# Gates of layer 1 in the ring of input tiles, the last two gate projections block by block, layer 1's weights loaded ahead

## The chip, the cores and the metric

The kernel runs on one core of a Trainium2 chip. The metric is the device time of one execution in microseconds (us). TensorE (PE) multiplies matrices into PSUM; VectorE (DVE) and ScalarE (ACT) do elementwise work and read PSUM; GpSimd (POOL) does elementwise work in SBUF; SyncE (SP) issues all of the kernel's DMA transfers, in order.

## The reference

Two encoder layers over 2048 tokens of width 1024. Each layer projects its modulated input, mixes it along time, multiplies the result with SiLU of gate columns, projects back and ends in a scaled residual and a layer norm. Layer 0 mixes with HGRN2 heads and RWKV7 heads; layer 1 with a gated linear recurrence (RG-LRU), which is the part that matters here:

```python
else:
    u = h @ od_w_in[o]
    xC, gC = jnp.split(u, 2, axis=-1)
    hC = rglru_branch(xC, od_conv_w[o], ...)   # conv of 4 taps, gates r and i, scan along time
    y = (hC * jax.nn.silu(gC.astype(f32))).astype(x.dtype) @ od_w_out[o]
x = layer_norm(DEEPNORM_ALPHA * x + (1.0 + gate[:, None]) * y, ln_g[l], ln_b[l])

# in rglru_branch
log_a = -C_POW * gate_r * jax.nn.softplus(-lam.astype(f32))
a = jnp.exp(log_a)
u = jnp.sqrt(-jnp.expm1(2.0 * log_a)) * (gate_i * xc)
_, h = lax.associative_scan(combine, (a, u), axis=1)
```

## The kernel before

Every product in f32 is made from three passes: both operands are split into a high part and a rest (split, L366 to L368: ACT casts the high part at L367, DVE or POOL subtracts the rest at L368), and mm3 (L430 to L433) issues low times high, high times high, high times low. A projection of 128 output columns is thus 24 matmuls of 128x512 for each half-block of 512 tokens.

Each layer runs over two super-blocks of 1024 tokens (sb = 0, 1), each of two half-blocks (b = 0, 1). The stages come as mix0_0, out0_0, mix0_1, out0_1, then mix1_0, out1_0, mix1_1, out1_1. A mix stage projects, mixes, and writes the mixed rows to o_dr in DRAM; its gate_steps (L551) projects the eight gate tiles k, multiplies each with its rows of o_dr, and writes the product to m_dr. An out stage (out_proj, L482) reads m_dr back as stationary operands (raw_mx), multiplies with the output weights (wo) and norms; beside it the next stage's inputs are prepared (out0_1 and out1_0 read them from x1_dr).

In mix1 (L1251) the eight conv inputs are projected two by two (pp_c, tiles u_c), and mix_c (L1092) treats each of four groups g: four conv steps into xc on ACT and DVE, a split of xc, 48 matmuls of the block-diagonal gates into pg_c, ACT's sigmoids gr and gi, and then, over the whole group at once, tanh, exp, square and sqrt on ACT and products on DVE, and at the end DVE's two scans into hc_c and their stores to o_dr. The tiles hc_c are of the tag c_o with two buffers; the gate tiles go of layer 1 have the same tag. The gate projections follow the groups in the program; a scheduler orders PE, ACT, DVE, POOL and SP by priority, which falls in program order but for blocks raised by high_priority, and fills PE's waits of mix_c with projections that are ready. In mix0 PE's order is written out by hand (manual_schedule), and the gates come at the end of it.

A gate's two half-blocks go to two PSUM blocks of the tag mm (two buffers), are copied by ACT to go (L574), put through SiLU (L564), multiplied on DVE with oi, the rows of o_dr (L568, loaded at L577), and stored to m_dr (L586). The last gate of a stage is not stored but split into tail tiles, half-block by half-block. The ring up (L101, 11 buffers of 515 f32 a partition) holds conv inputs u_c, oi, the tail tiles and gb, the broadcast output gate (L485).

Weights come through load_w, raw with two buffers, then high and low parts with four; load_w raises its priority by ahead. load_wo reads wo into tiles freed by the stage: in layer 0 two loads into the buffer of the tag sgi, which the last gate tile had, two into that of lr, which the gate before it had. An out stage's first matmul therefore stands behind the last gate's copy, SiLU, product and split, the load of wo, and wo's split.

Of the kernel before, what the change touches and what calls it, by code (L numbers as in the profile page):

```python
# [13 lines left out]
F32 = mybir.dt.float32  # L14
# [9 lines left out]
P = 128  # L24
D = 1024
KT = 8
BLK = 512
SBT = 1024
# [40 lines left out]
def tile_encoder(  # L69
# [47 lines left out]
    tp = _Cur()  # L117
    ps = ctx.enter_context(tc.tile_pool(name="ps", bufs=1, space=PSUM))
# [291 lines left out]
    def load_w(src, name, nk=KT, raws=None, ahead=0):  # L410
        with tc.high_priority(offset=ahead):
            return split_w(src, name, nk, raws)
# [17 lines left out]
    def mm3(pt, ah, al, bh, bl, first, last):  # L430
        nc.tensor.matmul(pt, ah, bl, start=first, stop=False)  # L431
        nc.tensor.matmul(pt, ah, bh, start=False, stop=False)  # L432
        nc.tensor.matmul(pt, al, bh, start=False, stop=last)  # L433

    def proj_steps(src, name, hs, evac, w=None):

        wh, wl = w or load_w(src, name)
        for b in range(2):
            pt = ps.tile([P, BLK], F32, name=f"pp_{name}_{b}", tag="mm", bufs=2)
            for k in range(KT):  # L440
                mm3(pt, wh[k], wl[k], hs[0][b][k], hs[1][b][k], k == 0, k == KT - 1)
                if k in (1, 3, 5):
                    yield
            evac(b, pt)
            yield

    def proj(*a):
        for _ in proj_steps(*a):
            pass

    def proj_start_steps(ws, hs):
# [96 lines left out]
            norm(j)  # L548
            after(j)

    def gate_steps(l, sb, hs, wsrc, ct0, order, tail, tags):  # L551


        def half(name, dt=F32):
            return up.tile([P, BLK + 3], dt, name=f"{name}_{l}_{sb}", tag="u")[:, 0:BLK]

        for n, k in enumerate(order):
            t0 = sb * SBT
            last = k == order[-1]
            go, oi = {}, {}  # L560

            def silu_mul(bs):
                for b in bs:
                    silu = nc.scalar.activation(go[b], go[b], AF.Silu)  # L564
                if l == 0:
                    ln_exp_after(silu)
                for b in bs:
                    nc.vector.tensor_mul(go[b], go[b], oi[b])  # L568

            def evac(b, pt):  # L570
                if b == 0:
                    g2 = tp.tile([P, 2, BLK], F32, name=f"go_{l}_{sb}_{k}", **tags[n % len(tags)])
                    go.update({0: g2[:, 0], 1: g2[:, 1]})
                nc.scalar.copy(go[b], pt)  # L574
                for j in (b,) if last else range(2) if b else ():
                    oi[j] = half(f"oi{k}_{j}")
                    nc.sync.dma_start(oi[j], o_dr[l][k, :, t0 + j * BLK : t0 + (j + 1) * BLK])  # L577
                if last:
                    silu_mul((b,))
                    hl = [half(f"m{i}_{b}", F32R) for i in range(2)]  # L580
                    split(hl[0], hl[1], go[b])
                    tail.append(hl)
                elif b:
                    silu_mul((0, 1))
                    for j in range(2):
                        nc.sync.dma_start(m_dr[l][k, :, t0 + j * BLK : t0 + (j + 1) * BLK], go[j])  # L586

            yield from proj_steps(wsrc[ct0(k)], f"g{l}_{sb}_{k}", hs, evac)


    a_state = [None] * 4
# [498 lines left out]
    c_state = [None] * 8  # L1090

    def mix_c(g, sb, us):  # L1092
        wh, wl = load_w(w_gate[g], f"wg{sb}_{g}")
        nm = f"c{g}_{sb}"
        xc = tp.tile([P, 2, SBT], F32, name=f"xc_{nm}", tag="c_x")
        gr = tp.tile([P, 2, SBT], F32, name=f"gr_{nm}", tag="c_gr")
        gi = tp.tile([P, 2, SBT], F32, name=f"gi_{nm}", tag="c_gi")
        for b in range(2):
            ls = slice(b * BLK, (b + 1) * BLK)
            xh = []  # L1100
            xl = []
            for i in range(2):
                ct = 2 * g + i
                u = us[i][b]
                x_ = xc[:, i, ls]
                nc.scalar.activation(
                    x_, u[:, 3 : BLK + 3], AF.Identity, scale=V("conv_w", 24 + ct), bias=V("conv_b", ct)
                )
                for w in range(3):
                    nc.vector.scalar_tensor_tensor(  # L1110
                        out=x_, in0=u[:, w : w + BLK], scalar=V("conv_w", 8 * w + ct), in1=x_,
                        op0=ALU.mult, op1=ALU.add,
                    )
                hi = tp.tile([P, BLK], F32R, name=f"xh{i}_{nm}_{b}", tag=f"c_h{i}", bufs=2)
                lo = tp.tile([P, BLK], F32R, name=f"xl{i}_{nm}_{b}", tag=f"c_l{i}", bufs=2)
                split(hi, lo, x_)
                xh.append(hi)
                xl.append(lo)
            for i in range(2):
                ct = 2 * g + i  # L1120
                for gt, t in enumerate((gr, gi)):
                    pt = ps.tile([P, BLK], F32, name=f"pg_{nm}_{b}_{i}_{gt}", tag="tb", bufs=2)
                    for k in range(2):
                        wi = gt * 4 + k * 2 + i
                        mm3(pt, wh[wi], wl[wi], xh[k], xl[k], k == 0, k == 1)
                    nc.scalar.activation(t[:, i, ls], pt, AF.Sigmoid, bias=V(("ba", "bx")[gt], ct))
        nc.vector.tensor_mul(gi, gi, xc)
        for i in range(2):
            nc.vector.tensor_scalar_mul(gr[:, i], gr[:, i], cv[:, 2 * g + i : 2 * g + i + 1])
        th = tp.tile([P, 2, SBT], F32, name=f"th_{nm}", tag="c_th")  # L1130
        nc.scalar.activation(th, gr, AF.Tanh, scale=-1.0)
        nc.scalar.activation(gr, gr, AF.Exp)
        nc.scalar.activation(xc, gr, AF.Square)
        nc.vector.scalar_tensor_tensor(out=th, in0=xc, scalar=1.0, in1=th, op0=ALU.add, op1=ALU.mult)
        nc.scalar.activation(th, th, AF.Sqrt)
        nc.vector.tensor_mul(gi, gi, th)
        for i in range(2):
            ct = 2 * g + i
            h = tp.tile([P, SBT], F32, name=f"hc{i}_{nm}", tag="c_o", bufs=2)
            init = 0.0 if c_state[ct] is None else c_state[ct]  # L1140
            nc.vector.tensor_tensor_scan(
                out=h, data0=gr[:, i], data1=gi[:, i], initial=init, op0=ALU.mult, op1=ALU.add
            )
            cs = sp_.tile([P, 1], F32, name=f"cs{i}_{nm}", tag=f"c_s{ct}", bufs=2)
            nc.gpsimd.tensor_copy(cs, h[:, SBT - 1 : SBT])
            c_state[ct] = cs
            nc.sync.dma_start(o_dr[1][ct, :, sb * SBT : (sb + 1) * SBT], h)
# [46 lines left out]
    def mix0(sb, hs, w_first):  # L1194


        lr = tp.tile([P, SBT], F32, name=f"lr{sb}", tag="lr")
        sgi_of, tail = {}, []
# [3 lines left out]
        def projections():  # L1202
            yield from low_rank(sb, hs, lr, w_first)
            for g in range(4):
                for i in range(3):
                    key = f"b{sb}_{i}_{g}"
                    yield from proj_steps(w_ev[16 + 4 * i + g], key, hs, evac_lerp(key, i, g, ub[g][i]))
                for i in (1, 2, 0):
                    ct = 4 * i + g
                    key = f"a{sb}_{ct}"  # L1210
                    yield from proj_steps(w_ev[ct], key, hs, evac_u(key, (0, ct), 0, ua[g][i]))
            yield from gate_steps(
                0, sb, hs, w_ev, lambda k: 12 + k if k < 4 else 28 + k, (0, 1, 2, 4, 5, 6, 3, 7), tail,
                [dict(tag="lr"), dict(tag="sgi")],
            )

        tasks = []
# [14 lines left out]
        with tc.manual_schedule(engines={nc.tensor.engine}):  # L1232
            while tasks or steps is not None:
# [3 lines left out]
                for entry in list(tasks):  # L1237
                    if entry[0] > now:
                        continue
                    if isinstance(entry[1], tuple):  # L1240
                        g, b, make, us = entry[1]
# [11 lines left out]
    def mix1(sb, hs, w_first):  # L1253
        for g in range(4):
            us = [[None, None] for _ in range(2)]
            for i in range(2):
                ct = 2 * g + i
                proj(
                    w_od[ct], f"c{sb}_{ct}", hs, evac_u(f"c{sb}_{ct}", (1, ct), 3, us[i]),
                    w_first[0] if ct == 0 else None,  # L1260
                )
            mix_c(g, sb, us)
        tail = []
        for _ in gate_steps(1, sb, hs, w_od, lambda k: 8 + k, range(KT), tail, [dict(tag="c_o", bufs=2)]):
            pass
        return tail, load_wo(1, sb, w_odo, [
            tp.tile([P, 4, BLK], F32, name=f"wo1_{sb}_{tag}", tag=tag) for tag in ("c_x", "c_gr", "c_gi", "c_th")
        ])
# [97 lines left out]
```

## Time and profile before

| what | value |
| --- | --- |
| median of 3 runs | 2450.46 us (2445.37 to 2455.84) |
| the profiled execution | 2446.24 us, span 2444.5 us |
| granted clock of PE, mean | 0.952 |
| PE busy | 2208.4 us, 90% |
| DVE, ACT, POOL busy | 60%, 51%, 23% |
| DMA, mean rate over the span | 94 GB/s |

The span is what the trace covers, and the profiled execution's own time lies 1.7 us above it. A busy share is an average over stages of different limits, and a matmul's row in a timeline overlaps the next one's, so that the distance of starts is its price. Idle time of an engine is shown at the instruction that ended it, with what released it.

### The profile page before, as it was taken

The page shows a single profiled execution, that of the slowest core. Times are in us where ns is not written, and L with a number is a line of the kernel's source. Part 1 is how long each engine was busy: PE and PEld are TensorE (multiplying, and loading weights), DVE is VectorE, ACT ScalarE, POOL GpSimd, SP SyncE. Part 2 cuts the span into 40 slices and gives each one's busy share as a digit, 9 for nine tenths or more (in the row PEclk, how much of TensorE's full clock was granted, in tenths as well). Part 3 has the DMA queues.
Part 4 walks back from the last instruction along what each step waited for, and adds up shares of the span by engine and source line. Part 5 has one row for each costly group of instructions (what it writes and reads, how often), then busy time and mean ns, then how long its engine had stood idle before and what let it go on. Part 6 is the DMA issues. An engine that isn't in the chain of part 4 may idle for free. (4 is left out here: it accounts for less than half of the span.)

```text
span 2444.5 us, 45532 instructions
## 1 busy us (share of the span) xinstructions
PE 2208.4 (90%) x18400; PEld 1738.7 (71%) x18400; DVE 1454.8 (60%) x2697; ACT 1256.6 (51%) x2027; POOL 557.2 (23%) x586
## 2 busy tenths in 40 slices
PE   5989989999987998899999999989986999996998
PEld 4767767677766876677776777768765778774776
DVE  6546667566644677565666755356766156766166
ACT  4344556545566433454455556654666344666332
POOL 3311112111112222111111111122433232433231
PEclk7989999999998999999999999989998999998999
DMA  7310111111424645111111123254313544113542
GB/s 289 93 37 24 41 32 41 38 38 38 118 70 128 207 152 175 34 34 43 25 42 35 37 83 97 72 204 143 104 65 120 169 141 137 67 57 122 167 137 103
DMA packets 185938, 229.82 MB, mean 94 GB/s; under 512 B 65912, under 2 KB 99320, under 8 KB 185728
## 3 DMA queue, kind: packets, MB, share of 16 engines
q1 hardware_dynamic: 185728, 226.92, 29.1%
q8 instruction: 144, 2.36, 0.4%
q14 instruction: 66, 0.54, 0.1%
HBM read 175.46 MB, written 51.39 MB: 93 GB/s over the span
## 5 line engine op out<-in xcount | busy, mean ns | idle before, releaser
L431 PE MATMUL pp_g<-hl_h,wh_g 128*128 128x512 f32 x512 | 212.3, 415 | 40.8 <-ACT go L574 40.8
L433 PE MATMUL pp_g<-hh_h,wl_g 128*128 128x512 f32 x512 | 204.6, 400 | 2.0 <-POOL wl_g L368 2.0
L431 PE MATMUL po<-hl_wo,wh_mx 128*128 128x512 f32 x448 | 179.3, 400 | 28.9 <-DVE hl_wo L368 24.1
L432 PE MATMUL pp_g<-hh_h,wh_g 128*128 128x512 f32 x512 | 204.9, 400 | 0.0
L433 PE MATMUL po<-hh_wo,wl_mx 128*128 128x512 f32 x448 | 177.4, 396 | 0.0
L432 PE MATMUL po<-hh_wo,wh_mx 128*128 128x512 f32 x448 | 177.2, 396 | 0.0
L368 POOL TENSOR_TENSOR wl_g<-raw_g,wh_g 128x512 fp32r<-128x512 f32 x64 | 87.2, 1363 | 377.5 <-ACT wh_g L367 342.7
L431 PE MATMUL pp_b<-hl_h,wh_b 128*128 128x512 f32 x384 | 168.5, 439 | 5.0 <-ACT cr_b L805 5.0
L431 PE MATMUL pp_a<-hl_h,wh_a 128*128 128x512 f32 x384 | 168.7, 439 | 0.0
L432 PE MATMUL pp_b<-hh_h,wh_b 128*128 128x512 f32 x384 | 153.7, 400 | 0.0
L433 PE MATMUL pp_a<-hh_h,wl_a 128*128 128x512 f32 x384 | 153.5, 400 | 0.0
L432 PE MATMUL pp_a<-hh_h,wh_a 128*128 128x512 f32 x384 | 153.3, 399 | 0.0
L433 PE MATMUL pp_b<-hh_h,wl_b 128*128 128x512 f32 x384 | 153.0, 398 | 0.0
L431 PEld LDWEIGHTS pp_g<-hl_h,wh_g 128*128 128x128 f32 x512 | 99.5, 194 | 64.7 <-ACT go L574 41.7
L368 POOL TENSOR_TENSOR wl_a<-raw_a,wh_a 128x512 fp32r<-128x512 f32 x48 | 67.7, 1416 | 329.1 <-ACT wh_a L367 329.1
L568 DVE TENSOR_TENSOR go<-go,oi 128x512 f32<-128x512 f32 x64 | 46.8, 733 | 160.6 <-ACT go L564 144.9
L368 POOL TENSOR_TENSOR wl_mx<-raw_mx,wh_mx 128x512 fp32r<-128x512 f32 x64 | 80.7, 1265 | 269.1 <-ACT wh_mx L367 269.1
L368 POOL TENSOR_TENSOR wl_b<-raw_b,wh_b 128x512 fp32r<-128x512 f32 x48 | 66.5, 1391 | 271.1 <-ACT wh_b L367 270.1
L431 PEld LDWEIGHTS po<-hl_wo,wh_mx 128*128 128x128 f32 x448 | 86.0, 192 | 48.4 <-DVE hl_wo L368 24.9
L433 PEld LDWEIGHTS pp_g<-hh_h,wl_g 128*128 128x128 f32 x512 | 99.2, 194 | 25.2 <-POOL wl_g L368 3.5
L432 PEld LDWEIGHTS pp_g<-hh_h,wh_g 128*128 128x128 f32 x512 | 99.4, 194 | 19.2
L433 PE MATMUL pp_c<-hh_h,wl_c 128*128 128x512 f32 x256 | 102.2, 400 | 8.6 <-POOL wl_c L368 8.6
(355 smaller groups left out, 5707.4 us busy)
## 6 DMA issues: line engine op xcount, KB each, us to landing
adw<-in_ada_w_dram SPq DMA_DIRECT2D x96, 256.0 KB
oi<-o_dr SPq DMA_DIRECT2D x64, 256.0 KB
m_dr<-go SPq DMA_DIRECT2D x56, 256.0 KB
raw_b<-in_w_ev_dram SPq DMA_DIRECT2D x48, 256.0 KB
raw_a<-in_w_ev_dram SPq DMA_DIRECT2D x48, 256.0 KB
raw_g<-in_w_ev_dram SPq DMA_DIRECT2D x32, 256.0 KB
wo<-in_w_evo_dram SPq DMA_DIRECT2D x32, 256.0 KB
raw_mx<-m_dr SPq DMA_DIRECT2D x32, 256.0 KB
```

The costliest lines, as they stand in the source:

```text
L368: return (eng or nc.vector).tensor_tensor(out=lo, in0=src, in1=hi.bitcast(F32), op=ALU.subtract)
L431: nc.tensor.matmul(pt, ah, bl, start=first, stop=False)
L432: nc.tensor.matmul(pt, ah, bh, start=False, stop=False)
L433: nc.tensor.matmul(pt, al, bh, start=False, stop=last)
L568: nc.vector.tensor_mul(go[b], go[b], oi[b])
```

## The change

Three things. The gate tiles of layer 1 no longer take the tag c_o: each half-block's go is a tile of the ring up. In every mix stage the last two gates (3 and 7 in layer 0, 6 and 7 in layer 1) load both weights first and then run half-block by half-block, first gate b = 0, second gate b = 0, first b = 1, second b = 1, with inputs, SiLU, product and store for each half-block. Layer 1's weights, of the conv inputs, of mix_c and of the gates, are loaded with ahead=100.

```diff
-    def proj_steps(src, name, hs, evac, w=None):
+    def proj_steps(src, name, hs, evac, w=None, ahead=0):
-        wh, wl = w or load_w(src, name)
+        wh, wl = w or load_w(src, name, ahead=ahead)
         for b in range(2):
...
+            yield from half_steps(wh, wl, name, hs, b, evac)
+
+    def half_steps(wh, wl, name, hs, b, evac):
+        pt = ps.tile([P, BLK], F32, name=f"pp_{name}_{b}", tag="mm", bufs=2)
+        for k in range(KT):
+            mm3(pt, wh[k], wl[k], hs[0][b][k], hs[1][b][k], k == 0, k == KT - 1)
+            if k in (1, 3, 5):
+                yield
+        evac(b, pt)
+        yield
...
             def evac(b, pt):
-                if b == 0:
-                    g2 = tp.tile([P, 2, BLK], F32, name=f"go_{l}_{sb}_{k}", **tags[n % len(tags)])
+                if b == 0 and l == 0:
+                    g2 = tp.tile([P, 2, BLK], F32, name=f"go_{l}_{sb}_{k}", tag=("lr", "sgi")[n % 2])
                     go.update({0: g2[:, 0], 1: g2[:, 1]})
+                if l:
+                    go[b] = half(f"go{k}_{b}")
                 nc.scalar.copy(go[b], pt)
-                for j in (b,) if last else range(2) if b else ():
+                bs = (range(2) if b else ()) if whole else (b,)
+                for j in bs:
                     oi[j] = half(f"oi{k}_{j}")
                     nc.sync.dma_start(oi[j], o_dr[l][k, :, t0 + j * BLK : t0 + (j + 1) * BLK])
-                if last:
-                    silu_mul((b,))
+                if len(bs):
+                    silu_mul(bs)
+                if k == order[-1]:
                     hl = [half(f"m{i}_{b}", F32R) for i in range(2)]
                     split(hl[0], hl[1], go[b])
                     tail.append(hl)
-                elif b:
-                    silu_mul((0, 1))
-                    for j in range(2):
+                else:
+                    for j in bs:
                         nc.sync.dma_start(m_dr[l][k, :, t0 + j * BLK : t0 + (j + 1) * BLK], go[j])
...
+        for n, k in enumerate(order[:-2]):
+            yield from proj_steps(wsrc[ct0(k)], f"g{l}_{sb}_{k}", hs, tile_evac(n, k, True), ahead=100 * l)
+
+        ws = [load_w(wsrc[ct0(k)], f"g{l}_{sb}_{k}", ahead=100 * l) for k in order[-2:]]
+        evacs = [tile_evac(KT - 2 + i, k, False) for i, k in enumerate(order[-2:])]
+        for b in range(2):
+            for i in range(2):
+                yield from half_steps(*ws[i], f"g{l}_{sb}_{order[KT - 2 + i]}", hs, b, evacs[i])
...
-        wh, wl = load_w(w_gate[g], f"wg{sb}_{g}")
+        wh, wl = load_w(w_gate[g], f"wg{sb}_{g}", ahead=100)
```

ACT behind group 3's block gates in mix1_0, before. In these names go_1_0_0 is gate 0 of layer 1 in super-block 0, c3_0 is group 3 in super-block 0, wh_g1_0_3_0 the first half of the weights of gate 3; the long number at the end only tells tiles apart, and a bracket names what a row waits for:

```order
L1126 ACTIVATE gi_c3_0_18775<-pg_c3_0_1_1_1_18864,vec_104 128x512 [waits PE_49]
L1131 ACTIVATE th_c3_0_18875<-gr_c3_0_18774 128x2048 [waits DVE_49]
L1132 ACT_TABLE_LOAD
L1132 ACTIVATE gr_c3_0_18774<-gr_c3_0_18774 128x2048 [waits Activation_49]
L1133 ACTIVATE xc_c3_0_18773<-gr_c3_0_18774 128x2048 [waits DVE_49,Activation_49]
L1135 ACT_TABLE_LOAD
L1135 ACTIVATE th_c3_0_18875<-th_c3_0_18875 128x2048 [waits DVE_49]
L574 COPY go_1_0_0_18929<-pp_g1_0_0_0_18904 128x512 [waits DMAHW4_49,DMAHW2_49,Pool_49]
L574 COPY go_1_0_0_18929<-pp_g1_0_0_1_18931 128x512
L564 ACT_TABLE_LOAD
```

And after, from the square on; go1_0 is half-block 0 of gate 1, go1_1 half-block 1, and L579 and L567 are the lines of the copy and of SiLU there:

```order
L1148 ACTIVATE xc_c3_0_18775<-gr_c3_0_18776 128x2048 [waits DVE_49,Activation_49]
L367 CAST wh_g1_0_3_1_19130<-raw_g1_0_3_1_19128 128x512 [waits DMAHW6_49,PE_49,Pool_49]
L579 COPY go1_1_1_0_19034<-pp_g1_0_1_1_19009 128x512 [waits PE_49]
L567 ACT_TABLE_LOAD
L567 ACTIVATE go1_0_1_0_19007<-go1_0_1_0_19007 128x512
L1150 ACT_TABLE_LOAD
L1150 ACTIVATE th_c3_0_18877<-th_c3_0_18877 128x2048 [waits DVE_49]
L567 ACT_TABLE_LOAD
L567 ACTIVATE go1_1_1_0_19034<-go1_1_1_0_19034 128x512 [waits Activation_49]
L367 CAST wh_g1_0_4_0_19200<-raw_g1_0_4_0_19198 128x512 [waits DMAHW7_49,PE_49,Pool_49]
L367 CAST wh_g1_0_4_1_19206<-raw_g1_0_4_1_19204 128x512 [waits DMAHW2_49,PE_49,Pool_49]
L579 COPY go2_0_1_0_19083<-pp_g1_0_2_0_19058 128x512
```

The copies of gate 0 are no longer here: they stand ahead of the group's first sigmoid and wait for PE alone. The second gate's copies, SiLU and the casts of gates 3 and 4 stand between the rows of mix_c, with four table loads from the exp's on, two before.

PE at the start of group 3's block gates in mix1_0, before:

```order
L431 MATMUL pp_g1_0_0_1_18931<-hl_h1_0_1_7_17767,wh_g1_0_0_1_18900 128x512
L432 MATMUL pp_g1_0_0_1_18931<-hh_h1_0_1_7_17751,wh_g1_0_0_1_18900 128x512
L433 MATMUL pp_g1_0_0_1_18931<-hh_h1_0_1_7_17751,wl_g1_0_0_1_18901 128x512
L431 MATMUL pg_c3_0_0_0_0_18792<-xl0_c3_0_0_18781,wh_wg0_3_0_18763 128x512
L432 MATMUL pg_c3_0_0_0_0_18792<-xh0_c3_0_0_18780,wh_wg0_3_0_18763 128x512
L433 MATMUL pg_c3_0_0_0_0_18792<-xh0_c3_0_0_18780,wl_wg0_3_0_18764 128x512
L431 MATMUL pg_c3_0_0_0_1_18800<-xl0_c3_0_0_18781,wh_wg0_3_1_18769 128x512
```

And after:

```order
L433 MATMUL pp_g1_0_1_0_18982<-hh_h1_0_0_1_17739,wl_g1_0_1_0_18973 128x512
L431 MATMUL pp_g1_0_1_0_18982<-hl_h1_0_0_2_17756,wh_g1_0_1_0_18972 128x512
L432 MATMUL pp_g1_0_1_0_18982<-hh_h1_0_0_2_17740,wh_g1_0_1_0_18972 128x512
L433 MATMUL pp_g1_0_1_0_18982<-hh_h1_0_0_2_17740,wl_g1_0_1_0_18973 128x512
L431 MATMUL pg_c3_0_0_0_0_18794<-xl0_c3_0_0_18783,wh_wg0_3_0_18765 128x512
L432 MATMUL pg_c3_0_0_0_0_18794<-xh0_c3_0_0_18782,wh_wg0_3_0_18765 128x512
L433 MATMUL pg_c3_0_0_0_0_18794<-xh0_c3_0_0_18782,wl_wg0_3_0_18766 128x512
L431 MATMUL pg_c3_0_0_0_1_18802<-xl0_c3_0_0_18783,wh_wg0_3_1_18771 128x512
```

Before, the 48 matmuls of pg_c follow gate 0 with no other between them, and gate 1 starts behind them. After, 9 matmuls of gate 1's first block stand ahead of the first pg_c, 6 and 8 more between the pieces that follow, and the last of its 24 behind pg_c; gate 1's second block and both of gate 2 come next.

SP at the start of out1_0, before:

```order
L420 DMA raw_mx_1_0_1_1_19643<-m_dr1_78 128x3x128
L577 DMA oi7_1_1_0_19490<-o_dr1_76 128x512
L420 DMA raw_mx_1_0_2_0_19799<-m_dr1_78 128x4x128
L420 DMA raw_mx_1_0_2_1_19805<-m_dr1_78 128x3x128
L485 DMA gb1_0_0_19589<-gate_dr1_82 128x512
L485 DMA gb1_0_1_19590<-gate_dr1_82 128x512
L386 DMA x1_1_0_0_19722<-x1_dr_79 128x1024
L386 DMA x1_1_0_1_19724<-x1_dr_79 128x1024
L386 DMA x1_1_0_2_19726<-x1_dr_79 128x1024
```

And after:

```order
L420 DMA raw_mx_1_0_2_0_19809<-m_dr1_78 128x4x128
L583 DMA oi7_1_1_0_19500<-o_dr1_76 128x512
L420 DMA raw_mx_1_0_2_1_19815<-m_dr1_78 128x3x128
L386 DMA x1_1_0_0_19732<-x1_dr_79 128x1024
L386 DMA x1_1_0_1_19734<-x1_dr_79 128x1024
L488 DMA gb1_0_0_19599<-gate_dr1_82 128x512
L488 DMA gb1_0_1_19600<-gate_dr1_82 128x512
L386 DMA x1_1_0_2_19736<-x1_dr_79 128x1024
L386 DMA x1_1_0_3_19738<-x1_dr_79 128x1024
```

Two of the loads x1 of the next stage's input, 512 KB each, now stand ahead of gb.

## Rows read from the trace of the kernel before

**Rows 1.** Waits of PE: engine, line, releaser: us in total, times, longest.

```profile
PE pp_g L431 <- ACT go L574: 40.8, 2, 20.4
...
PE po L431 <- DVE hl_wo L368: 24.1, 2, 12.2
...
PE pp_c L433 <- POOL wl_c L368: 8.6, 4, 2.2
```

**Rows 2.** PE timeline, first layer-1 stage: start, us, instruction, [idle before, releaser].

```profile
1862.39 0.66 PE L431 MATMUL pg_c<-xl_c,wh_wg 128*128 128x512 f32 x1 [2.10 <-DVE xl_c L368]
...
1869.32 0.75 PE L431 MATMUL pg_c<-xl_c,wh_wg 128*128 128x512 f32 x1 [2.23 <-ACT gr_c L1126]
...
1879.15 0.40 PE L433 MATMUL pg_c<-xh_c,wl_wg 128*128 128x512 f32 x1
1899.94 0.79 PE L431 MATMUL pp_g<-hl_h,wh_g 128*128 128x512 f32 x1 [20.39 <-ACT go L574]
```

**Rows 3.** PE timeline, first and last of 19 matmuls in a clean run.

```profile
773.65 0.39 PE L433 MATMUL pp_g<-hh_h,wl_g 128*128 128x512 f32 x1
...
777.73 0.39 PE L433 MATMUL pp_g<-hh_h,wl_g 128*128 128x512 f32 x1
```

**Rows 4.** Windows: us, busy us of each engine (instructions), PEclk, DMA share, GB/s.

```profile
1900.00:1903.20 3.20, 3.20 (x8) 2.52 (x9) 0.80 (x2) 2.81 (x4) 0.00 (x0) 0.50 0.90 258
1904.00:1910.00 6.00, 6.00 (x28) 4.95 (x27) 0.69 (x1) 1.33 (x3) 0.00 (x0) 1.00 0.96 297
```

**Rows 5.** ACT timeline across the long wait of rows 2.

```profile
1880.51 1.91 ACT L1131 ACTIVATE th_c<-gr_c 128x2048 f32<-128x2048 f32 x1
1882.44 1.28 ACT L1132 ACT_TABLE_LOAD   x1
1883.73 1.91 ACT L1132 ACTIVATE gr_c<-gr_c 128x2048 f32<-128x2048 f32 x1
...
1889.94 1.91 ACT L1135 ACTIVATE th_c<-th_c 128x2048 f32<-128x2048 f32 x1 [1.06 <-DVE th_c L1134]
1899.30 1.07 ACT L574 COPY go<-pp_g 128x512 f32<-128x512 f32 x2 [7.45 <-DMA o_dr<-hc_c]
...
1901.69 1.15 ACT L564 ACTIVATE go<-go 128x512 f32<-128x512 f32 x2
```

**Rows 6.** DVE timeline, from group 2's scans to group 3's first product.

```profile
1851.82 5.49 DVE L1141 TENSOR_TENSOR_SCAN hc_c<-gr_c,gi_c 128x1024 f32<-128x1024 f32 x2
1857.23 4.50 DVE L1110 SCALAR_TENSOR_TENSOR xc_c<-u_c,vec,xc_c 128x512 f32<-128x512 f32 x5
1861.65 0.68 DVE L368 TENSOR_TENSOR xl_c<-xc_c,xh_c 128x512 fp32r<-128x512 f32 x1
```

**Rows 7.** PE timeline at projection 6, first layer-1 stage.

```profile
1810.39 0.50 PE L431 MATMUL pp_c<-hl_h,wh_c 128*128 128x512 f32 x1 [1.57 <-ACT wh_c L367]
...
1813.53 0.50 PE L433 MATMUL pp_c<-hh_h,wl_c 128*128 128x512 f32 x1 [2.18 <-POOL wl_c L368]
```

**Rows 8.** SP timeline at the end of mix0_0.

```profile
784.27 0.82 SPq L474 DMA_DIRECT2D wo<-in_w_evo_dram  x2
```

**Rows 9.** PE timeline at the end of mix0_0.

```profile
790.06 0.79 PE L431 MATMUL po<-hl_wo,wh_mx 128*128 128x512 f32 x1 [11.94 <-DVE hl_wo L368]
```

**Rows 10.** SP timeline at the end of mix1_0.

```profile
1987.25 3.39 SPq L386 DMA_DIRECT2D x<-x_dr  x6
```

**Rows 11.** PE timeline, out1_0, ahead of its third block.

```profile
1991.63 0.50 PE L431 MATMUL po<-hl_wo,wh_mx 128*128 128x512 f32 x1 [2.61 <-DVE y L508]
```

**Rows 12.** Chain of waits, out1_0: start, us, what.

```profile
1986.18 4.61 DMA gb<-gate_dr
```

**Rows 13.** Waits of ACT, columns as in rows 1.

```profile
ACT go L574 <- PE pp_g L433: 88.8, 27, 5.5
```

**Rows 14.** Page, part 5: group, then busy us, mean ns, idle before.

```profile
L568 DVE TENSOR_TENSOR go<-go,oi 128x512 f32<-128x512 f32 x64 | 46.8, 733 | 160.6 <-ACT go L564 144.9
```

**Rows 15.** Chain of waits, second layer-1 stage: the store behind the wait.

```profile
2261.98 2.61 DMA o_dr<-hc_c
```

More of the change, by code (lines that the diff above doesn't have):

```diff
@@ L433, in mm3, with proj @@
         nc.tensor.matmul(pt, al, bh, start=False, stop=last)
-    def proj_steps(src, name, hs, evac, w=None):
-        wh, wl = w or load_w(src, name)
+    def proj_steps(src, name, hs, evac, w=None, ahead=0):
+        wh, wl = w or load_w(src, name, ahead=ahead)
         for b in range(2):
[L439 to L448, printed above, removed]
+            yield from half_steps(wh, wl, name, hs, b, evac)
[7 more added lines that the diff above has]
+        yield
+    def proj(*a, **k):
+        for _ in proj_steps(*a, **k):
             pass
@@ L549, in out_proj, with gate_steps, tile_evac @@
             after(j)
-    def gate_steps(l, sb, hs, wsrc, ct0, order, tail, tags):
+    def gate_steps(l, sb, hs, wsrc, ct0, order, tail):
         def half(name, dt=F32):
             return up.tile([P, BLK + 3], dt, name=f"{name}_{l}_{sb}", tag="u")[:, 0:BLK]
-        for n, k in enumerate(order):
-            t0 = sb * SBT
-            last = k == order[-1]
+        t0 = sb * SBT
+        def tile_evac(n, k, whole):
             go, oi = {}, {}
@@ L582, in evac @@
                     tail.append(hl)
-                elif b:
-                    silu_mul((0, 1))
-                    for j in range(2):
+                else:
+                    for j in bs:
                         nc.sync.dma_start(m_dr[l][k, :, t0 + j * BLK : t0 + (j + 1) * BLK], go[j])
-            yield from proj_steps(wsrc[ct0(k)], f"g{l}_{sb}_{k}", hs, evac)
+            return evac
+        for n, k in enumerate(order[:-2]):
[5 more added lines that the diff above has]
+                yield from half_steps(*ws[i], f"g{l}_{sb}_{order[KT - 2 + i]}", hs, b, evacs[i])
     a_state = [None] * 4
@@ L1212, in projections @@
             yield from gate_steps(
-                0, sb, hs, w_ev, lambda k: 12 + k if k < 4 else 28 + k, (0, 1, 2, 4, 5, 6, 3, 7), tail,
-                [dict(tag="lr"), dict(tag="sgi")],
+                0, sb, hs, w_ev, lambda k: 12 + k if k < 4 else 28 + k, (0, 1, 2, 4, 5, 6, 3, 7), tail
             )
@@ L1259, in mix1 @@
                     w_od[ct], f"c{sb}_{ct}", hs, evac_u(f"c{sb}_{ct}", (1, ct), 3, us[i]),
-                    w_first[0] if ct == 0 else None,
+                    w_first[0] if ct == 0 else None, ahead=100,
                 )
@@ L1263, in mix1 @@
         tail = []
-        for _ in gate_steps(1, sb, hs, w_od, lambda k: 8 + k, range(KT), tail, [dict(tag="c_o", bufs=2)]):
+        for _ in gate_steps(1, sb, hs, w_od, lambda k: 8 + k, range(KT), tail):
             pass
```

## The prediction

> **What bounds the kernel now.** TensorE (PE) is busy nine tenths of the span, so I read first the view of who waited for whom on PE. Its longest entry is two waits of 20.4 us, one in each layer-1 stage: the gate projections (pp_g) wait for ACT's copy of a gate block out of PSUM [rows 1]. The second thing to see is two waits of about 12 us at the ends of the layer-0 stages, and the third the waits for weights at projection 6 (8.6 us over four). The rest of PE's waits is small or lies where the change moves nothing.
>
> Then the timelines of that place in the first layer-1 stage. PE issues the last product of group 3's block gates (pg_c) at 1879.15 and stands until 1899.94 [rows 2]. Both PSUM blocks of the tag mm hold gate 0, unread. ACT is in order: it runs tanh, a table load, exp, square, a table load, sqrt, then stands 7.45 us before the first gate copy, released by the store of hc_c [rows 5]: the gate tile shares its two buffers with the scans' outputs, and those must have been stored. The copy is thus the last link of a chain that runs from pg_c over tanh, sqrt, DVE's scans and a store, which itself took 2.61 us to land in the other stage [rows 15]. Ahead of it PE also stood 2.10 us for xl_c and 2.23 us for ACT's gr_c [rows 2].
>
> Prices. Nineteen matmuls of a clean run start between 773.65 and 777.73 [rows 3]: 4.08/18 = 0.227 us each. Behind the long wait the granted clock was 0.50, which is 1.2 GHz, for a window of 3.2 us with 8 matmuls, then 1.00, which is 2.4 GHz [rows 4]. Eight at 0.40 instead of 0.227 cost 1.4 us, once behind a wait. On ACT, tanh to table 1.93, table to exp 1.29, a gate copy 1.07/2 = 0.53, a silu 1.15/2 = 0.58, and from a copy's start to the waiting matmul 0.64 [rows 2, 5]. I price a weight cast like a copy of the same size, 0.53.
>
> **Change part 1: gate tiles in the ring, weights ahead (layer 1).** The copy of gate 0 no longer needs hc_c's buffers. In the new order PE runs both blocks of gate 0, then 23 of the 24 matmuls of gate 1's first block between the pieces of pg_c, and behind pg_c only 1 + 24 + 24 + 24 = 73 matmuls before it needs a third PSUM turn, for gate 3. ACT has both copies of gate 0 ahead of the first sigmoid, waiting for PE alone.
>
> Call T the end of pg_c: 1879.15 + 0.23 = 1879.4 before. Where does it go? DVE's rows before it stand end to end, scans, five conv steps, the first xl_c [rows 6], so PE's start on pg_c hangs on DVE and not on PE. Two more gate products of 0.73 us [rows 14] now stand on DVE ahead of the second half of group 3. That alone gives 1879.4 + 1.5 = 1880.9. The other end: 48 pg_c and 14 matmuls put between them, from 1862.39 on without a hole, end at 1862.39 + 62 x 0.227 = 1876.5. I take 1880, nearer to the first, because the chain has no slack in rows 6.
>
> From T, ACT in its new order: tanh starts at T + 1.1 (1880.51 in rows 5). Then tanh, exp, square and sqrt 4 x 1.93 = 7.7, four table loads 4 x 1.29 = 5.2 (two before), two copies and four casts 6 x 0.53 = 3.2, two silu 1.2: the copy that PE needs (gate 2, first block) starts at T + 18.4, and PE goes on at T + 19.0. PE reaches that point at T + 73 x 0.227 = T + 16.6. So a wait of 2.4 us stays in place of 20.4, and its half clock, 1.4.
>
> Compare at one piece of work, the end of gates 0 to 2 with PE free. Of their 144 matmuls 48 lie before T before, and 71 after. Before: 1899.94 + 96 x 0.227 + 1.4 = 1923.1. After: 1880 + 19.0 + 1.4 = 1900.4. Gain **22.7 us in a stage, 45.4 in two** (the second repeats it, rows 1). The gain is not that the copy comes sooner, T + 19.0 against T + 20.5; it is that 96 matmuls are done by then. What covers the new work on ACT: 27 gate copies waited for PE, 88.8 us in all [rows 13], so behind this place ACT is early. Three instructions more cost nothing there.
>
> The weights ahead: ACT casts projection 6's weights before an evacuation that they stood behind, so the waits of 1.57 and 2.18 us [rows 7] go. I count them at nothing, because PE then reaches pg_c of the next groups sooner and waits there for DVE's chain; if the chain gave way, they bring 3.7 a stage. SP's queue is passed by hc_c's stores ahead of gate 2's second input and gate 5's weights; those are needed 16 us and more later, against a landing of 2.61 [rows 15].
>
> Bounds for a stage: best, T at 1876.5 and all of rows 7, 22.7 + 3.5 + 3.7 = 30; worst, T at 1881 and every table switch at twice its row, 22.7 - 1 - 5.2 = 16.5.
>
> On those table switches the rows show the next ACTIVATE 1.29 us behind the start of the load, and the load 1.93 behind a tanh of 1.91 [rows 5]: nothing is drained beside. The Trainium skill (ScalarE: Activation LUTs, What ACT_TABLE_LOAD costs) adds a drain of about 1.38 us to each switch, 2.66 in all, and so speaks against a change that adds switches. By it, an estimate, the wait of 2.4 would be 7.9 and the sum 11 us worse; this case's trace disagrees with it, at 1.29.
>
> **Part 2: the last two gates block by block.** The matmuls are the same and in a row. Layer 0's tails: PE waits 11.94 us [rows 9] for the last gate's chain: its copy, silu and split free the buffer for two wo loads at 784.27 [rows 8], which are cast and split before PE goes on. The last block is still last, so the chain stays. Two casts move ahead of its copy, 2 x 0.53 = 1.1, and SP gets two loads, 0.41 each by rows 8, ahead of wo: +1.9, I take **+2 in each of two tails, +4**. The near end is 0 (they fit in waits), the far one a load of gb's landing, 4.61 [rows 12], so 5 each. Layer 1, first stage: out1_0 waits 2.61 us for y [rows 11] because gb landed 4.61 us after its issue [rows 12]. Two x1 loads of 512 KB now go ahead of gb: 2 x 3.39/6 = 1.1 of issue [rows 10], up to 4.6 more if they take the DMA engines as gb's own load did. I take **+3**, between. In the second stage no next layer loads, 0.
>
> **Sum.** -45.4 + 4 + 3 = **-38.4 us**. Against the profiled execution's 2446.24 that is 2407.8; this execution lies 4.2 below the median, so I forecast 2450.46 - 38.4 = **2412 us**. All bounds good, -60 + 0 + 1.1, give 2391; all bad, -33 + 10 + 5.7, give 2433.
>
> **Rivals.**
> 1. *The chain gives way as well*: T early, projection 6's waits gained. For it: the filled holes also take away two half-clock stretches. Against: rows 6. -2 x (26 to 30) + 7: about 2400.
> 2. *ACT's queue becomes the wait*: each added switch costs double, or a cast waiting for PE stands before the copy. For it: ACT is in order, and the cast of gate 4's weights stands before the copy that PE wants; against: 1.29 in rows 5. With four switches at 1.29 more, 2.4 becomes 7.6: -45.4 + 10.4 + 7 = -28, 2422. The skill's drain, cited above, lands at the same place, 2423.
> 3. *It doesn't do what it says*: the ring has 11 slots, and the copy of gate 0 waits for a slot as it did for hc_c. Then 40.8 stays and the tails' +7 is left: 2457. Against: in the new order the copy waits for PE alone, the slots before it held conv inputs that DVE has read.
> 4. *Slower: the ring holds the gates.* Each gate takes four of 11 slots, and a second input load waits for the store of the gate two before it. If that store and load come in line with PE, each of the 24 gate blocks left (12 a stage) pays one landing, 2.61 [rows 15]: -38 + 63 = +25, 2475. It decides from (38 + 12)/24 = 2.1 us a block. Against: a gate's two blocks are 48 x 0.227 = 10.9 us of PE, and ACT waits for PE in rows 13.
>
> **Chances.** Forecast (2404 to 2418) 0.55, rival 1 0.18, rival 2 (2418 to 2438) 0.18, rival 3 0.05, rival 4 0.04. The range of 2391 to 2433 holds the first three but for a rest. Half a per cent, 12 us, is about what a measurement of this kernel tells from no change: faster 0.91, same 0.05, slower 0.04.
>
> **What the profile after would show.** Right: the wait of pp_g for the gate copy is under 4 us in each stage, 73 matmuls lie between pg_c and it, pp_g of gate 1 fills the waits for xl_c and gr_c. Wrong: a wait of pp_g over 7 us (rival 2), or one of 20 (rival 3); waits of pp_g spread over gates 3 to 7 (rival 4); PE's 12 us at the layer-0 tails over 17, or out1_0's 2.61 over 9, which would eat the gain from behind.

## The result, and the profile after

The changed kernel takes 2414.2 us (median of 4 runs, 2409.88 to 2416.55), the kernel before 2447.9 (4 runs). The ratio of the mean times is 0.9856, with a 95% interval of 0.9826 to 0.9885: 1.4% faster. Forecast were 2412 us, with a range of 2391 to 2433. The profiled execution took 2413.01 us, its span 2411.3; the granted clock of PE was 0.957 (0.952 before).

The waits of PE in the changed kernel, columns as in rows 1:

```profile
PE po L431 <- DVE hl_wo L368: 29.2, 2, 14.7
...
PE po L431 <- DVE y L511: 9.2, 2, 5.1
...
PE pp_g L431 <- ACT go L579: 4.0, 2, 2.0
```

The 40.8 us for the gate copy are 4.0 now; the layer-0 tails went from 24.1 to 29.2, and the waits for y at the starts of layer 1's out stages from 4.8 to 9.2, by this line of before:

```profile
PE po L431 <- DVE y L508: 4.8, 2, 2.6
```

The next rows are the place of rows 2 on PE: first product of group 3's block gates, the last one, the last matmul before the wait, and what follows it.

```profile
1872.71 0.50 PE L431 MATMUL pg_c<-xl_c,wh_wg 128*128 128x512 f32 x1 [1.64 <-DVE xl_c L368]
...
1887.04 0.40 PE L433 MATMUL pg_c<-xh_c,wl_wg 128*128 128x512 f32 x1
...
1903.62 0.39 PE L433 MATMUL pp_g<-hh_h,wl_g 128*128 128x512 f32 x1
1906.02 0.50 PE L431 MATMUL pp_g<-hl_h,wh_g 128*128 128x512 f32 x1 [2.01 <-ACT go L579]
```

And ACT there, which answers to rows 5:

```profile
1888.41 1.93 ACT L1146 ACTIVATE th_c<-gr_c 128x2048 f32<-128x2048 f32 x1
...
1890.82 1.28 ACT L1147 ACT_TABLE_LOAD   x1
1892.11 1.92 ACT L1147 ACTIVATE gr_c<-gr_c 128x2048 f32<-128x2048 f32 x1
...
1897.36 1.28 ACT L567 ACT_TABLE_LOAD   x1
...
1899.30 1.28 ACT L1150 ACT_TABLE_LOAD   x1
...
1902.53 1.28 ACT L567 ACT_TABLE_LOAD   x1
...
1905.39 1.06 ACT L579 COPY go<-pp_g 128x512 f32<-128x512 f32 x2
```

The copy is still behind the whole chain of tanh, exp, square and sqrt, 33 us after PE's first product of the group; but it waits for no store, and PE works for 16.6 us of the time in which it stood before.

Where the time went, by stage, each from its first matmul to the next stage's first (the first pp_z, pp_c or po in the PE timelines; us):

| stage | before | after | difference |
| --- | --- | --- | --- |
| before mix0_0 | 34.96 | 34.21 | -0.8 |
| mix0_0 | 755.10 | 757.90 | +2.8 |
| out0_0 | 89.90 | 90.25 | +0.4 |
| mix0_1 | 736.30 | 741.57 | +5.3 |
| out0_1 | 96.39 | 97.45 | +1.1 |
| mix1_0 | 265.27 | 240.76 | -24.5 |
| out1_0 | 99.18 | 100.60 | +1.4 |
| mix1_1 | 266.11 | 243.84 | -22.3 |
| out1_1 | 101.29 | 104.72 | +3.4 |
| span | 2444.5 | 2411.3 | -33.2 |

Layer 1's mix stages gave 46.8 us, and 13.6 were given back elsewhere. Mix0 without its tail is the same work in both kernels.

### The profile page after: what moved, and what is told of

The parts are those of the page before. It is cut to its first block, busy times and chain, and to the rows that moved or that the text cites. A ratio compares the mean times of both kernels' runs of the same rounds, so it can differ in the third digit from the quotient of the medians.

```text
span 2411.3 us, 45519 instructions
## 1 busy us (share of the span) xinstructions
PE 2208.4 (92%) x18400; PEld 1738.2 (72%) x18400; DVE 1457.2 (60%) x2697; ACT 1265.7 (52%) x2035; POOL 554.9 (23%) x586
## 5 line engine op out<-in xcount | busy, mean ns | idle before, releaser
L431 PE MATMUL po<-hl_wo,wh_mx 128*128 128x512 f32 x448 | 180.2, 402 | 38.3 <-DVE hl_wo L368 29.2
L368 POOL TENSOR_TENSOR wl_g<-raw_g,wh_g 128x512 fp32r<-128x512 f32 x64 | 96.9, 1519 | 349.3 <-ACT wh_g L367 289.3
```

The lines of the kernel that those rows point to most:

```text
L368: return (eng or nc.vector).tensor_tensor(out=lo, in0=src, in1=hi.bitcast(F32), op=ALU.subtract)
```

## The experiments

The first five kernels take the change apart. A time given for a stage is that of the one profiled execution of its kernel.

Only the ring (no half-block order, no weights ahead):

```diff
-        for n, k in enumerate(order[:-2]):
-            yield from proj_steps(..., tile_evac(n, k, True), ahead=100 * l)
-        ws = [load_w(...) for k in order[-2:]]
-        ...
+        for n, k in enumerate(order):
+            yield from proj_steps(..., tile_evac(n, k, n < KT - 1), ahead=0)
...
-        wh, wl = load_w(w_gate[g], f"wg{sb}_{g}", ahead=100)
+        wh, wl = load_w(w_gate[g], f"wg{sb}_{g}")
...
-                    w_first[0] if ct == 0 else None, ahead=100,
+                    w_first[0] if ct == 0 else None,
```

> Only the gate tiles of layer 1 go to the ring; the last two gates run one after the other and the weights are loaded without a raise, as before. Theory A (the shared buffer of hc_c and the gate tiles made the wait of 20.4 us): the wait for the gate copy falls under 4 us in each layer-1 stage, 13 of gate 1's matmuls lie between the pieces of pg_c; 38 to 46 us less than before, the layer-0 tails keep their 12 us, so 2403 to 2412. Rival B (the weights ahead make the room): the wait stays over 10 us in each stage and the time within 25 us of before, 2423 to 2448.

Measured: 2398.4 us, ratio 0.9800 (0.9774 to 0.9826), faster than the whole change (the two intervals meet at 0.9826). Its mix1 stages take 239.0 and 239.1 us, and its list of PE's waits has no wait for a gate copy. Of gate 1's first block 11 matmuls were left behind pg_c, so 11 + 72 = 83 matmuls, 18.8 us at 0.227, cover the way to the copy of gate 2. Theory A holds and its sum was too small: the two mix1 stages alone are 53.3 us shorter than before. The other two parts of the change together cost something.

The ring and the weights ahead, without the half-block order (the first hunk above, with ahead=100 * l):

> The change without the half-block order of the last two gates. Theory A with the tails as counted: the two layer-0 tails go back from 14.5 to 12 us each, which is 5 us less than the changed kernel, 2406 to 2412. Rival: the half-block order shortens layer 1's end by as much as it costs layer 0, and the time is that of the changed kernel, 2414.

Measured: 2402.3 us, 0.9808 (0.9779 to 0.9837), below the range. Its waits:

```profile
PE po L431 <- DVE hl_wo L368: 23.8, 2, 11.9
PE pp_c L433 <- POOL wl_c L368: 9.6, 5, 3.1
PE po L431 <- DVE y L511: 5.9, 2, 2.9
PE pp_g L431 <- ACT go L579: 4.1, 2, 2.0
```

The tails are back at 11.9 and the waits for y at 2.9: the half-block order, on the ring, costs 5.4 us at layer 0's tails and 3.3 at layer 1's out stages in these lists. The out stages as a whole, 100.6 and 103.7 us, are only 1.0 us shorter than in the changed kernel. Between this kernel and the ring alone the times do not separate, but the lists differ by the wait for the copy, 4.1 against none.

A tag of their own for the gate tiles, in the kernel before, and nothing else:

```diff
-        for _ in gate_steps(..., tail, [dict(tag="c_o", bufs=2)]):
+        for _ in gate_steps(..., tail, [dict(tag="c_go", bufs=2)]):
```

> The kernel before with one edit: the gate tiles of layer 1 have a tag of their own with two buffers instead of hc_c's. Theory A: the same 20.4 us wait goes as with the ring, 38 to 46 us less than before, 2402 to 2410. Rival C (the ring's many half tiles are needed, two whole tiles of two halves hold the copies back): a wait for a gate tile's store comes in place of the old, over 5 us in a stage, and the gain is under 30 us.

Measured: 2399.8 us, 0.9800 (0.9774 to 0.9826), 2 us under the range; mix1 stages 238.8 and 239.2, and no wait for a gate copy. One word does what the ring does. The shared buffers were the whole cause of rows 1's first line, and two gate tiles are enough.

The other two parts with the gate tiles left where they were:

```diff
-                if b == 0 and l == 0:
-                    g2 = tp.tile(..., tag=("lr", "sgi")[n % 2])
-                if l:
-                    go[b] = half(f"go{k}_{b}")
+                if b == 0:
+                    kw = dict(tag="c_o", bufs=2) if l else dict(tag=("lr", "sgi")[n % 2])
+                    g2 = tp.tile(..., **kw)
```

> The change with the gate tiles left in hc_c's buffers: half-block order and weights ahead alone. Theory A: the waits of 20.4 us stay, the layer-0 tails cost 5 us, the weights ahead bring at most 3 us a stage: 2446 to 2456, same as before. Rival B: over 15 us faster than before.

Measured: 2446.9 us, 0.9994 (0.9982 to 1.0007), no difference, with these waits:

```profile
PE pp_g L431 <- ACT go L578: 41.5, 2, 21.1
PE po L431 <- DVE hl_wo L368: 26.6, 2, 13.4
```

The long wait stays as theory A said. But no wait for y is in that list: out1_0 takes 94.5 us and out1_1 97.8, 4.7 and 3.5 less than before. So the half-block order seems to help layer 1's ends when the gate tiles are not in the ring (this kernel loads the weights ahead as well; a pair below separates the two). What it gains is lost elsewhere: 2.5 us in the tails, 1.3 in mix1_1, and in this execution 4.9 in mix0_0, of which the tail explains 1.4.

The change without the weights ahead (ahead=0 everywhere):

> The change without the weights ahead. Theory A, from the stages of the ring alone: the layer-1 mix stages fall from 240.8 and 243.8 to about 239 each, since gate 1 covers the copy of gate 2 then and the wait of 3.1 us for projection 6's low weights in the second stage goes; the tails stay: 2406 to 2411, 4 to 8 us under the changed kernel. Rival: the weights ahead bring something, without them 2414 or more.

Measured: 2404.6 us, 0.9808 (0.9786 to 0.9830), mix1 stages 239.5 and 239.9, no wait for the copy; a little under the range. The stages are 1.3 and 4.0 us shorter than in the changed kernel. By its trace the second holds a wait for the low part of a conv weight that is longer than any of that kind in rows 1 (2.2):

```profile
2166.97 0.80 PE L433 MATMUL pp_c<-hh_h,wl_c 128*128 128x512 f32 x1 [3.10 <-POOL wl_c L368]
```

All the kernels with the raise have this wait of 3.1 us, those without have none above 2.2, so the raise makes it; why it leaves POOL later at that place was not tried. That the raise costs 1.3 and 4.0 us is not shown. The ring of 8 below has the raise, the same wait of 3.1 and the same waits for the copy, and its stages take 238.7 and 239.4 us: what differs from the changed kernel is the granted clock, 1.00 and 0.99 against 0.99 and 0.97. (Here it is 0.97 in both stages, with less waiting.) In the first stage the four kernels with the raise and without the shared buffers take 238.7 to 240.8 us, those without the raise (the ring alone, the own tag, this one) 238.8 to 239.5, which is no difference. In the second those without take 239.1 to 239.9, and three of the four with it 242.7 to 244.2. By the times this kernel and the changed one just touch (0.9830 and 0.9826), and the ring alone does not separate from the ring with the weights ahead.

Next, what the half-block order loses. A ring of 8 in the changed kernel:

```diff
-    up = ctx.enter_context(tc.tile_pool(name="up", bufs=11))
+    up = ctx.enter_context(tc.tile_pool(name="up", bufs=8))
```

> The change with a ring of 8 buffers instead of 11; layer 0 uses the ring too, so read the layer-1 mix stages by themselves, 240.8 and 243.8 us with 11. Theory A (a slot is free two gates, some 22 us, before it is wanted): within 3 us of that. Rival D (the ring holds the gates): each of the last 12 blocks waits for a landing, 10 us or more longer in each of these stages.

Measured: 2407.2 us, 0.9842 (0.9815 to 0.9868); mix1 stages 238.7 and 239.4, 2.1 and 4.5 us less than with 11, by the granted clock as said above. Rival D falls: even 8 slots hold no gate back. But the waits for y grow with the smaller ring, to 5.6 and 6.8:

```profile
PE po L431 <- DVE y L511: 12.3, 2, 6.8
```

gb in a tag of its own, with a ring of 9 to make room:

```diff
-        gb = [up.tile([P, BLK + 3], F32, ..., tag="u")[:, 0:BLK] for n in range(2)]
+        with tc.high_priority(offset=150):
+            gb = [up.tile([P, BLK], F32, ..., tag="gb", bufs=2) for n in range(2)]
```

> The change with gb in a tag of its own and a raised priority, the ring cut from 11 to 9 buffers to make room. Theory A (out1's wait for y is gb, which SP issues late): the waits for y, 4.1 and 5.1 us, go, with their half clock 9 to 12 us less than the changed kernel, 2402 to 2406; the ring of 9 holds nothing back in layer 1. Rival: the waits for y stay or move, 2412 to 2418.

Measured: 2390.9 us, 0.9772 (0.9745 to 0.9799). No wait for y is left; out1_0 takes 94.8 and out1_1 97.9, 12.6 us less than in the changed kernel. The time lies further down than was expected: by the traces another 3.7 us came from the layer-0 tails, 2.7 from the mix1 stages, and 6.7 from the rest of layer 0. Layer 0 uses the ring too, so how much of that is the edit and how much the spread between executions is not shown. The edit joins three things (tag, priority, ring). A smaller ring alone made the waits longer, so tag or priority frees gb; which of the two, this does not show.

Then the useful parts together. Own tag for the gates, half-block order in layer 1 alone, no weights ahead:

> The gate tiles of layer 1 in a tag of their own, the half-block order of the last two gates in layer 1 alone, no weights ahead. Theory A, from the stages of the runs so far: layer-1 mix stages of 239 us as with the own tag, out1_0 and out1_1 near 94.5 and 98 as in the run of the half-block order without the ring (there gb came early and the wait for y was gone), layer-0 tails 12 us: 5 to 9 us under the own tag's 2400, 2389 to 2396. Rival: the half-block order of layer 1 brings nothing once the gates are early, 2397 to 2402.

Measured: 2386.6 us, 0.9751 (0.9721 to 0.9781), with out1 stages of 97.1 and 97.5 and no wait for y, better than was expected. The own tag alone, which differs by the half-block order of layer 1, has 102.4 and 101.6, with 4.1 us of waits for y: this pair shows that the half-block order helps layer 1's ends. gb is issued 3.6 us into each out stage here, and 8.2 us there.

And with layer 0's last gate in two tiles of the ring:

```diff
+                if l == 0 and k == order[-1]:
+                    go[b] = half(f"go{k}_{b}")
+                elif b == 0:
```

> As the kernel before it in this call, and layer 0's last gate in tiles of the ring instead of the buffer that the first two loads of wo need. Theory A (the same fault in layer 0: a buffer that a late chain frees holds a load back): the two waits of 12 us for hl_wo fall under 4 us each, 16 to 24 us less than the kernel before it, 2368 to 2380. Rival (the load of wo is late for another reason, SP's order or the last split): the waits stay over 8 us and the gain is under 8 us.

Measured: 2375.1 us, 0.9708 (0.9681 to 0.9735), 11.4 us less where 16 to 24 were expected. The waits for hl_wo fall from 12 us to 1.2, and others come in their place:

```profile
PE po L431 <- ACT go L580: 9.1, 2, 4.8
...
PE po L431 <- DVE hl_wo L368: 2.3, 2, 1.2
```

So the buffer that held the load of wo was about half of the tail. The other half is a wait for the last gate's copy. By the kernel, po and the gate take their PSUM blocks from the tag mm, which has two; that po waits for such a block is read from that and not shown. In mix0_0 the copy starts at 780.35, 3.7 us behind PE's last product: ACT first treats the first half-block (SiLU, a table load, 1.35 us of waiting for DVE's product, casts). Whether a third block would shorten the wait was not tried. mix0_0 fell by 12.7 us and mix0_1 by 16.2; out0_0 grew by 5.7 and out0_1 by 7.2.

Last, that kernel with gb's own tag and a ring of 9:

> Gate tiles of layer 1 in a tag of their own, half-block order in layer 1, layer 0's last gate in the ring, and gb in its own tag with a raised priority and a ring of 9: all that helped so far. If the gains add, 2362 to 2374. Rival: gb was already in time in the half-block order of layer 1, and the ring of 9 gains nothing: 2374 to 2380.

Measured: 2376.5 us, 0.9698 (0.9677 to 0.9719), the same as without. The rival holds: gb was in time already.

## Why the prediction was right, step by step

**The wait and its place: right.** T, the end of pg_c, was expected 0.6 us later in the stage than before; it came at 1887.27 - 1721.38 = 165.9 us from the stage's first matmul, against 166.7 before: 0.8 earlier, within the bounds. ACT's copy was put at T + 18.4 and started at T + 18.1; a wait of 2.4 was left by the sum, and 2.01 and 2.04 us were measured. The gain of a stage was put at 22.7 and was 24.5 and 22.3. Behind T the two stages agree: 23.7 and 23.6 us against 23.3 in the sum (22.7 and the 0.6 by which T was to come later). The rest is T, 0.8 earlier in the first stage and 1.3 later in the second.

**The table switches: right, by the row and not by the page.** The next ACTIVATE starts 1.29 us behind the load's start, as in rows 5 (1890.82 and 1892.11 above). With the drain of 1.38 us that the Trainium skill (ScalarE: Activation LUTs, What ACT_TABLE_LOAD costs) adds to each switch, the wait would have been 7.9 us, an estimate. This trace disagrees with it: the measurement decides, and four switches cost what rows 5 said.

**The weights ahead, counted at nothing: right in the first stage, and missed in the second.** The cast of projection 6's weights was no longer behind the evacuation, and in the first stage the raise did not move T, as was argued: it lies 165.4 to 165.9 us into the stage in the four kernels with the raise and no shared buffer, 165.6 to 166.2 in the three without the raise. But POOL's low parts came late, which was not in the sum. In the second stage PE waited 3.10 us for them, half clock (a granted clock of 0.50) followed, and T came 1.3 us later than before; in the ring of 8 no half clock followed the same wait, and T came at 166.0 and not at 169.0. The last wait of 2 us belongs to the raise as well: without it 83 matmuls and not 73 stand behind pg_c, and PE's cover is as long as ACT's chain. By itself that wait costs next to nothing, because the ten matmuls that no longer cover it, 2.3 us, are done ahead of T. From T to the end a stage takes 73.2 and 73.0 us without the raise, and 73.3 and 73.4 in the ring of 8 with raise and wait. The changed kernel takes 74.9 twice, with half clock behind the wait.

**Layer 0's tails, +2 each: right in size, wrong in the step.** The waits are 2.55 and 2.51 us longer. But the last gate's copy is hardly later: it starts 0.44 us behind the end of PE's run before (778.12) and 0.80 behind it after (777.62), 0.4 more where 1.1 was counted. The new rows of ACT:

```profile
778.42 0.57 ACT L579 COPY go<-pp_g 128x512 f32<-128x512 f32 x1
...
785.55 0.62 ACT L367 CAST hh_wo<-wo 128x512 fp32r<-128x512 f32 x1 [2.16 <-DMA wo<-in_w_evo_dram]
787.82 3.22 ACT L367 CAST hh_wo<-wo 128x512 fp32r<-128x512 f32 x6 [1.66 <-DMA wo<-in_w_evo_dram]
```

Before, ACT ran eight casts there without a gap, and waited for one load alone:

```profile
783.43 4.25 ACT L367 CAST hh_wo<-wo 128x512 fp32r<-128x512 f32 x8
788.75 0.62 ACT L367 CAST hh_wo<-wo 128x512 fp32r<-128x512 f32 x1 [1.07 <-DMA wo<-in_w_evo_dram]
```

The buffer of lr is freed a block later in the half-block order, and its two loads of wo are late with it. Before, they were issued here:

```profile
772.71 0.46 SPq L474 DMA_DIRECT2D wo<-in_w_evo_dram  x1
...
774.09 0.48 SPq L474 DMA_DIRECT2D wo<-in_w_evo_dram  x1
```

And after:

```profile
782.33 0.95 SPq L477 DMA_DIRECT2D wo<-in_w_evo_dram  x2
```

The two loads of sgi's buffer, which the sum was about, are issued at 784.14 against 784.27. So six casts stand in line behind two waits.

**out1_0 and out1_1, +3 and 0: the mechanism right in the first, the second missed.** The first wait for y grew by 1.5 us and the second by 2.9, the stages by 1.4 and 3.4. In the first the sum counted a later issue of gb and a slower landing. The issue was not later, 7.71 us into the stage against 8.26; the landing took 6.63 us against 4.61 in rows 12. In the second it took 6.13 against 4.15 before. Two rows of the chain of waits in the changed kernel:

```profile
1969.84 6.63 DMA gb<-gate_dr
...
2315.71 6.13 DMA gb<-gate_dr
```

And the second stage before:

```profile
2351.46 4.15 DMA gb<-gate_dr
```

In the second stage no x1 is loaded, and I took that for no cost; two loads of the residual rows, as large, stand ahead of gb there:

```profile
2314.86 0.81 SPq L495 DMA_DIRECT2D r<-x_dr  x2
2315.71 0.91 SPq L488 DMA_DIRECT2D gb<-gate_dr  x2
```

Nor did I ask what sets the issue of gb. It sits in the same ring as the gate tiles now. The waits for y are 9.2 us in a ring of 11 and 12.3 in a ring of 8. With gb in the ring of 11 but the gate tiles out of it, the half-block order has gb issued 3.6 us into the stage, and no wait for y is left.

**What the sum missed.** The spans differ by 33.2 us, 5.2 less than the 38.4 summed. That 2414 us lies 2 us from the forecast is in part luck: the kernel before came out 2.5 us under the median from which the forecast was counted. 46.8 came from layer 1's mix (45.4 summed); 13.6 were lost (7 summed), of which 5.1 lie in the tails, 4.8 in the out1 stages and some 4 in the same work of layer 0. The latter can't be told from the spread between executions: the kernels with the same mix0_0 take 751.7 to 758.8 us for it.

## What to carry to other kernels

A tile that waits for a buffer belongs to the chain of whoever had the buffer before: look at which tags two producers share, and give the later one its own before moving work. Work that is moved from behind a long wait into short waits ahead of it no longer covers the long one; here the two cancelled, 2.3 us of matmuls against a wait of 2.0, so sum both sides. And a ring that everything shares moves the wait to its least urgent user; here that was a small broadcast at the start of the next stage.

## What the runs showed that was not expected

The same 7340 matmuls of mix0_0, in the same order, took from 751.7 us (the ring alone) to 758.8 (the own tag) in different executions, more than most of the terms of the sum. PE's idle gaps in them add up to 72.1 and 73.0 us, so most of the difference lies in the granted clock, 0.94 and 0.93. The tables by stage, more than the totals, separated edits of a few us, but a stage differs by its clock too: in mix1_1 the rings of 11 and 8 have nearly the same waits, 14.8 and 15.2 us in all, and take 243.8 and 239.4 us.

A wait of only 2.01 us was followed by the half clock in the changed kernel: the starts behind it lie 0.33 and 0.34 us apart, and then the rows lengthen; from 1907.1 to 1909.6 the granted clock was 0.50.

```profile
1906.35 0.54 PE L432 MATMUL pp_g<-hh_h,wh_g 128*128 128x512 f32 x1
1906.69 0.63 PE L433 MATMUL pp_g<-hh_h,wl_g 128*128 128x512 f32 x1
```

With the ring of 8 the same wait, 2.00 us, was not followed by it: the rows stay at 0.40, and from 1901.3 to 1903.8 the granted clock was 1.00.

```profile
1901.06 0.50 PE L431 MATMUL pp_g<-hl_h,wh_g 128*128 128x512 f32 x1 [2.00 <-ACT go L579]
1901.40 0.40 PE L432 MATMUL pp_g<-hh_h,wh_g 128*128 128x512 f32 x1
1901.64 0.40 PE L433 MATMUL pp_g<-hh_h,wl_g 128*128 128x512 f32 x1
```

So the half clock that the prediction counted behind its remaining wait, 1.4 us, may come or not; what decides it these runs do not show.
